# A decoder layer with sparse attention on one core: a 64-row product made one of 128 rows

## The chip, the cores and the metric

The kernel runs on one core of a Trainium2 chip. The metric is device time in microseconds for one execution. Before the change it is 919.27 us, the median of three runs (918.22 to 921.02).

## The reference

One layer of a decoder on 512 positions of width 1024: a combined input projection, a short convolution as one mixer, an attention with 16 heads (4 for keys and values, head size 64) as the other, a gated merge, and a SwiGLU block. The attention has three branches, each with keys and values of its own:

```python
p_cmp = masked_softmax(s, cmp_end[None, :] <= t[:, None])      # over 31 compressed blocks
o_cmp = einsum('bhgqn,bhnd->bhgqd', p_cmp, v_cmp)
...                                                            # selected blocks, window
o = einsum('bsch,cbshd->bshd', br_gates, o_all)                # gated sum of the three
```

The compressed branch reduces 512 positions to 31 blocks per head, kept as 32 columns (NB) of which the last is masked. Its product with the values, o_cmp, is what the change touches.

## The kernel before, in words

All matrix products use operands split in two parts (high and low, H and L), and add three products of the parts on TensorE in `mm` (lines 119 to 121). Weights come by DMA as `raw`, and ACT (line 95) and VectorE or GpSimd (line 96) split them.

The attention runs as 32 units: 8 pairs of heads (`pr`) by 4 tiles of 128 positions (`i`). The order of TensorE is the order of the program; for the other engines a planner sets the order, and `tc.high_priority` moves an instruction ahead in it. A unit goes through `slot(u)`: the scores of the next unit (`score`, matmuls of line 497), then the transposes of the compressed probabilities (`trans(u, -1)`, line 550) and of the first 128 columns of the two other branches (`trans(u, 0)`, four transposes of line 564), then two steps of filling work (`fl`, each step three matmuls of 512 columns of some other product), then `pv(u, -1, t)`, which is line 577. Then come, for each further tile j up to i, transposes, a filling step, and the products of lines 582 and 583 with the values of the two other branches; for i = 0 the scores of the unit after the next follow line 577 at once. `o_out` reads the sum (lines 591 and 594).

For the compressed branch the transposed probabilities of the two heads are 64 rows: rows 0 to 31 and 32 to 63. ACT copies the high parts into a tile (line 555, two instructions of 32 x 128), and VectorE puts the low parts into the other 32 rows of the same columns (line 557, two instructions). So one product with a stationary tile of 64 rows, `VC`, that holds the values twice, adds high and low parts. `VC` is made once, in `v_cmp` (lines 318 to 322), after the hidden layer of the compression has been transposed into `gh` and `gl`.

The tile for the transposed probabilities comes from the pool `th`, which has two buffers (`THB`); both the compressed step and each step j take one in turn. The low parts of the steps j go to `tl`, also two buffers (lines 567 and 568).

Of the kernel before, what the change touches and what calls it, by code (L numbers as in the profile page):

```python
# [8 lines left out]
F32R = mybir.dt.float32r  # L9
# [4 lines left out]
P = 128  # L14
S = 512
# [5 lines left out]
KVH = 4  # L21
NB = 32
# [9 lines left out]
def f(ap):  # L32
    return ap.bitcast(F32)

PTB = 5
THB = 2
# [10 lines left out]
def body(tc, a):  # L47
    with tc.manual_schedule(engines={mybir.EngineType.PE}):
        trace(tc, a)


def trace(tc, a):
    nc = tc.nc
    es = ExitStack()

    def pool(stack, **kw):
        return stack.enter_context(tc.tile_pool(**kw))
# [59 lines left out]
    def mm(ps, lhs, rhs, first, last):  # L117

        nc.tensor.matmul(ps, lhs[0], rhs[0], start=first, stop=False)  # L119
        nc.tensor.matmul(ps, lhs[0], rhs[1], start=False, stop=False)  # L120
        nc.tensor.matmul(ps, lhs[1], rhs[0], start=False, stop=last)  # L121
# [18 lines left out]
    kvp = pool(kvst, name="kvp", bufs=1, side="left")  # L140
# [4 lines left out]
        KH[ct] = kp.tile([P, 2, KC], F32R, name=f"KH{ct}")  # L145
        KL[ct] = kp.tile([P, 2, KC], F32R, name=f"KL{ct}")
    VT = kvp.tile([P, NT, 2, KVH, P], F32R, name="VT")
    VC = kvp.tile([2 * NB, KVH, P], F32R, name="VC")

    pst = ExitStack()  # L150
    ps1 = pool(pst, name="ps1", bufs=1, space=PSUM)
# [4 lines left out]
    def tp_tile():  # L156
        return ps1.tile([P, S], F32, name="tp", bufs=2)
# [4 lines left out]
    def av_tile():  # L162
        return ps1.tile([P, S], F32, name="av")

    oyst = ExitStack()
    oyp = pool(oyst, name="oyp", bufs=1, side="right")
# [20 lines left out]
    for k in range(KD):  # L187
# [10 lines left out]
        if 3 <= k < 3 + NT:  # L198
            t = k - 3
# [109 lines left out]
    def v_cmp(gT, w):  # L309
        ps = tp_tile()  # L310
        o = ps[:, 0:HD]
        for c in range(2):
            cc = slice(c * P, (c + 1) * P)
            wc_ = slice(c * HD, (c + 1) * HD)
            mm(o, (gT[0][:, cc], gT[1][:, cc]), (w[0][:, wc_], w[1][:, wc_]), c == 0, c == 1)
        for g in range(KVH):
            src = o[g * NB:(g + 1) * NB]
            nc.scalar.activation(VC[0:NB, g, 0:HD], src, AF.Copy, scale=0.5)
            nc.vector.scalar_tensor_tensor(VC[0:NB, g, HD:P], in0=src, scalar=0.5,
                                           in1=f(VC[0:NB, g, 0:HD]), op0=ALU.mult,  # L320
                                           op1=ALU.subtract)
        nc.vector.tensor_copy(VC[NB:2 * NB], f(VC[0:NB]))

    vps = {}

    def v_proj(br, kh):
# [145 lines left out]

    units = [(pr, i) for pr in range(8) for i in range(NT)]
    U = {}

    def scores(u):
        pr, i = units[u]
        g = pr // 2
        q = Q[pr]
        qs = slice(i * P, (i + 1) * P)  # L480
        w = (i + 1) * P
        ncol = NB + 2 * w
        b0 = S - NB - 2 * P
        pieces = [(0, 288)]
        c0 = 288
        while c0 < ncol:
            n = min(512, ncol - c0)
            pieces.append((c0, n))
            c0 += n
        U[u] = dict(pts=[], nms=[], w=w,  # L490
                    pc=ap_.tile([P, 2, NB], F32, name="pc", bufs=3))
        for h in range(2):
            ps = sc_tile()
            for c0, n in pieces:
                o = ps[:, b0 + c0:b0 + c0 + n]
                for j, kk in enumerate((KH, KL)):
                    nc.tensor.matmul(o, q[:, h, qs], kk[g // 2][:, g % 2, c0:c0 + n],  # L497
                                     start=(j == 0), stop=(j == 1))

            nr = nrs8[:, i:i + 1]  # L500
            pt = ap_.tile([P, 2 * S], F32, name="pt", bufs=PTB)
            nm = ap_.tile([P, 3], F32, name="nm", bufs=4)
            sv = ps[:, S - 2 * P:S - 2 * P + 2 * w].rearrange("p (j b c) -> p b j c", b=2, c=P)
            nc.vector.tensor_tensor_reduce(
                out=U[u]["pc"][:, h], in0=ps[:, b0:b0 + NB], in1=cmsk[:, i], scale=nr,
                scalar=TOP, op0=ALU.add, op1=ALU.min, accum_out=nm[:, 0:1])
            for b in range(2):
                r0 = b * S
                nc.vector.tensor_tensor_reduce(  # L509
                    out=pt[:, r0:r0 + w].rearrange("p (j c) -> p j c", c=P),  # L510
                    in0=sv[:, b], in1=tri[:, NT - 1 - i:NT], scale=nr, scalar=TOP,
                    op0=ALU.add, op1=ALU.min, accum_out=nm[:, b + 1:b + 2])
            U[u]["pts"].append(pt)
            U[u]["nms"].append(nm)
            yield

    def expo(u, h):
        pr, i = units[u]
        if h == 0:
            U[u]["sm"] = ap_.tile([P, 2, 3], F32, name="sm", bufs=3)  # L520
        pt, nm = U[u]["pts"][h], U[u]["nms"][h]
        for b in range(3):
            s = U[u]["pc"][:, h] if b == 0 else pt[:, (b - 1) * S:(b - 1) * S + U[u]["w"]]
            nc.scalar.activation(s, s, AF.Exp,  # L524
                                 scale=-1.0, bias=nm[:, b:b + 1],
                                 accum_out=U[u]["sm"][:, h, b:b + 1])
# [17 lines left out]
    def trans(u, j):  # L544
        pts = U[u]["pts"]
        tp = tp_tile()
        th = ap_.tile([P, S], F32R, name="th", bufs=THB)
        if j < 0:

            nc.tensor.transpose(tp[0:2 * NB, 0:P], U[u]["pc"].rearrange("p h n -> p (h n)"), ident)  # L550
            with tc.high_priority(PRI):
                rows = [slice(0, NB), slice(NB, 2 * NB)]
                cols = [slice(0, P), slice(P, 2 * P)]
                for h in range(2):
                    nc.scalar.activation(th[rows[h], cols[h]], tp[rows[h], 0:P], AF.Copy)
                for h in range(2):
                    nc.vector.tensor_tensor(th[rows[1 - h], cols[h]], tp[rows[h], 0:P],
                                            f(th[rows[h], cols[h]]), op=ALU.subtract)
            return th, None
        tl = ap_.tile([P, S], F32R, name="tl", bufs=THB)  # L560
        for b in range(2):
            for h in range(2):
                r0 = b * S + j * P
                nc.tensor.transpose(tp[:, (2 * b + h) * P:(2 * b + h + 1) * P],  # L564
                                    pts[h][:, r0:r0 + P], ident)
        with tc.high_priority(PRI):
            nc.scalar.activation(th, tp, AF.Copy)  # L567
            nc.vector.tensor_tensor(tl, tp, f(th), op=ALU.subtract)  # L568
        return th, tl

    def pv(u, j, t):
        pr, i = units[u]
        g = pr // 2
        if j < 0:
            U[u]["av"] = av_tile()[:, 0:256]
            av = U[u]["av"]
            nc.tensor.matmul(av, VC[:, g], t[0][0:2 * NB, 0:256], start=True, stop=False)  # L577
            return
        av = U[u]["av"]
        for b in range(2):  # L580
            bs = slice(b * 256, (b + 1) * 256)
            nc.tensor.matmul(av, VT[:, j, b, g], t[0][:, bs], start=False, stop=False)  # L582
            nc.tensor.matmul(av, VT[:, j, b, g], t[1][:, bs], start=False,  # L583
                             stop=(j == i and b == 1))
# [16 lines left out]
    ap_ = pool(ast, name="ap", bufs=2, side="right", reuse_waits="tile")  # L601
# [89 lines left out]
    def score(u, h):  # L691
        if u >= NU:
            return
        if h == 0:
            SC[u] = scores(u)
        next(SC[u])

    def slot(u):
# [11 lines left out]
        score(u + 1, 1)  # L710
        fl(F0[i])
        t = trans(u, -1)
        tn = trans(u, 0)
        if u + 1 < NU:
            expo(u + 1, 1)
        fl(F1[i])
        pv(u, -1, t)
        for j in range(1, i + 1):
            t, tn = tn, trans(u, j)
            fl(1)  # L720
            pv(u, j - 1, t)
            if j == 1:
                score(u + 2, 0)
# [4 lines left out]
        if u + 2 < NU:  # L728
            expo(u + 2, 0)
        fl(left)  # L730
        pv(u, i, tn)
        o_out(u)

# [6 lines left out]
    gvT = gelu_T(gv)  # L740
    fill.step(3)
    v_cmp(gvT, w2v)
    score(1, 0)
    expo(1, 0)
    fill.step(PRE)
# [332 lines left out]
```

## Time and profile before

| | before |
|---|---|
| median of three runs | 919.27 us (918.22 to 921.02) |
| profiled execution | 917.53 us, its span 915.7 us |
| TensorE matmul, busy | 898.8 us, 98% of the span |
| TensorE weight load, busy | 760.2 us, 83% |
| VectorE, busy | 515.5 us, 56% |
| ACT, busy | 426.3 us, 47% |

Busy time of TensorE is not a measure of its pace: matmuls overlap, so that 0.39 us of a 512-column matmul are followed by the next after 0.23. Weight loads (PEld) are separate rows, and normally run beside the matmul before them. What a product costs is read from the start of one matmul to the start of the next.

### The profile page before, as it was taken

How to read it: one execution, taken by the hardware profiler on the slowest of the kernel's cores; microseconds unless marked ns; L12 is line 12 of the kernel's file. 1: busy time of each engine (PE TensorE's matmuls, PEld its weight loads, DVE VectorE, ACT ScalarE, POOL GpSimd, SP SyncE). 2: the span in 40 equal slices, each digit the busy share in tenths (PEclk: the TensorE clock that was granted, in tenths of full speed). 3: DMA queues.
4: the chain of work that ended last, by engine and by line, in shares of the span. 5: the costliest groups of instructions: out<-in, count | busy, mean ns of one | idle time of the engine just before them, and what ended most of it. 6: DMA issues, size and time to landing. Idle time of an engine off the chain costs nothing.

```text
span 915.7 us, 12776 instructions
## 1 busy us (share of the span) xinstructions
PE 898.8 (98%) x4757; PEld 760.2 (83%) x4757; DVE 515.5 (56%) x1217; ACT 426.3 (47%) x936; POOL 119.6 (13%) x79
## 2 busy tenths in 40 slices
PE   9889999999999999999999999999999999999996
PEld 7789788888888888878888999888888888888885
DVE  4896788888888788775455452333333333223223
ACT  6446776767767777664333522332223222212212
POOL 1000424232242222330000300000000000000100
PEclk9999999999999999999999999999999999999999
DMA  9244511211112111114523700223333323332212
GB/s 313 70 119 162 161 47 50 67 47 53 65 46 71 47 52 65 47 64 150 178 92 97 235 16 24 93 92 92 100 108 92 92 93 103 102 94 92 93 47 92
DMA packets 26270, 85.14 MB, mean 93 GB/s; under 512 B 3424, under 2 KB 3680, under 8 KB 26208
## 3 DMA queue, kind: packets, MB, share of 16 engines
q1 hardware_dynamic: 24912, 82.78, 28.5%
q10 hardware_dynamic: 1296, 1.55, 0.5%
q8 instruction: 37, 0.61, 0.3%
q14 instruction: 25, 0.20, 0.1%
HBM read 82.23 MB, written 2.10 MB: 92 GB/s over the span
## 4 chain that ended last, share of the span: by engine, by line
PE 88%; DVE 6%; DMA 2%; ACT 2%; issue 1%; SPq 0%; POOL 0%; POOLq 0%; ACTq 0%; DVEq 0%
PE acc L119 24%; PE acc L121 24%; PE acc L120 24%; PE sc L497 4%; PE tp L564 4%; PE av L582 2%; PE av L583 2%; DVE blk L249 2%; DVE wl L96 1%; PE av L577 1%; DMA w2kr<-w2k 1%; DMA raw<-wk 1%; ACT wh L95 1%; DMA xT<-xT 0%; DMA xt<-x 0%
## 5 line engine op out<-in xcount | busy, mean ns | idle before, releaser
L95 ACT ACTIVATE wh<-raw 128x1024 fp32r<-128x1024 f32 (+2 forms) x143 | 144.6, 1013 | 314.4 <-PE acc L120 117.0
L119 PE MATMUL acc<-nH,wh 128*128 128x512 f32 x656 | 262.3, 400 | 0.0
L121 PE MATMUL acc<-nH,wl 128*128 128x512 f32 x656 | 256.1, 390 | 0.0
L120 PE MATMUL acc<-nL,wh 128*128 128x512 f32 x656 | 256.1, 390 | 0.0
L96 DVE TENSOR_TENSOR wl<-raw,wh 128x1024 fp32r<-128x1024 f32 (+2 forms) x107 | 123.4, 1154 | 170.1 <-ACT wh L95 170.0
L121 PEld LDWEIGHTS acc<-nH,wl 128*128 128x128 f32 x656 | 123.1, 188 | 26.8 <-POOL wl L96 0.4
L119 PEld LDWEIGHTS acc<-nH,wh 128*128 128x128 f32 x656 | 123.4, 188 | 21.4
L120 PEld LDWEIGHTS acc<-nL,wh 128*128 128x128 f32 x656 | 123.5, 188 | 21.2
L96 POOL TENSOR_TENSOR wl<-raw,wh 128x1024 fp32r<-128x1024 f32 x36 | 86.6, 2407 | 236.7 <-DVE pt L540 96.4
L121 PE MATMUL acc<-wh,aL 128*128 128x512 f32 (+1 forms) x198 | 73.4, 371 | 0.0
L119 PE MATMUL acc<-wh,aH 128*128 128x512 f32 (+1 forms) x198 | 73.4, 371 | 0.0
L120 PE MATMUL acc<-wl,aH 128*128 128x512 f32 (+1 forms) x198 | 73.4, 370 | 0.0
L524 ACT ACTIVATE pt<-pt,nm 128x128 f32<-128x128 f32 (+3 forms) x128 | 70.7, 554 | 2.6 <-DVE nm L509 2.0
L509 DVE CUSTOM_DVE_ANT_0 pt<-sc,tri,nrs 128x128 f32<-128x128 f32 (+3 forms) x128 | 65.4, 545 | 0.1
L568 DVE TENSOR_TENSOR tl<-tp,th 128x512 fp32r<-128x512 f32 x80 | 55.1, 689 | 13.0 <-ACT th L567 11.3
L915 DVE TENSOR_TENSOR sg<-acc,sg 128x512 f32<-128x512 f32 x22 | 15.2, 691 | 81.0 <-PE acc L121 81.0
L567 ACT ACTIVATE th<-tp 128x512 fp32r<-128x512 f32 x80 | 47.4, 592 | 13.2 <-PE tp L564 12.1
L564 PE MATMUL tp<-ident,pt 128*128 128x128 f32 x320 | 49.7, 277 | 0.1
L961 POOL TENSOR_TENSOR h<-h,gfin 128x512 f32<-128x512 f32 x4 | 6.0, 1542 | 299.1 <-ACT jk L943 299.1
L120 PEld LDWEIGHTS acc<-wl,aH 128*128 128x128 f32 x198 | 37.3, 188 | 7.1
L119 PEld LDWEIGHTS acc<-wh,aH 128*128 128x128 f32 x198 | 37.3, 188 | 7.1
L121 PEld LDWEIGHTS acc<-wh,aL 128*128 128x128 f32 x198 | 37.3, 188 | 7.0
(229 smaller groups left out, 1496.9 us busy)
## 6 DMA issues: line engine op xcount, KB each, us to landing
raw<-wg SPq DMA_DIRECT2D x22, 512.0 KB, 3.5
raw<-wu SPq DMA_DIRECT2D x22, 512.0 KB, 3.5
raw<-wd SPq DMA_DIRECT2D x22, 512.0 KB, 3.5
raw<-wcv SPq DMA_DIRECT2D x12, 512.0 KB, 3.6
raw<-wq SPq DMA_DIRECT2D x8, 512.0 KB, 3.6
raw<-w SPq DMA_DIRECT2D x8, 512.0 KB, 3.5
raw<-wgc SPq DMA_DIRECT2D x8, 512.0 KB, 3.5
raw<-wga SPq DMA_DIRECT2D x8, 512.0 KB, 3.5
```

The costliest lines, as they stand in the source:

```text
L95: nc.scalar.activation(h[:, :n], raw[:, :n], AF.Copy)
L96: ins = (eng or nc.gpsimd).tensor_tensor(l[:, :n], raw[:, :n], f(h[:, :n]), op=ALU.subtract)
L119: nc.tensor.matmul(ps, lhs[0], rhs[0], start=first, stop=False)
L120: nc.tensor.matmul(ps, lhs[0], rhs[1], start=False, stop=False)
L121: nc.tensor.matmul(ps, lhs[1], rhs[0], start=False, stop=last)
L249: nc.vector.tensor_tensor(blk[lp * HD:(lp + 1) * HD, :, 2 * ct + hp, 0:NB - 1], src, pos, op=ALU.add)
L497: nc.tensor.matmul(o, q[:, h, qs], kk[g // 2][:, g % 2, c0:c0 + n], start=(j == 0), stop=(j == 1))
L509: nc.vector.tensor_tensor_reduce(out=pt[:, r0:r0 + w].rearrange("p (j c) -> p j c", c=P), in0=sv[:, b], in1=tri[:, NT - 1 - i:NT], scale=n ...
L524: nc.scalar.activation(s, s, AF.Exp, scale=-1.0, bias=nm[:, b:b + 1], accum_out=U[u]["sm"][:, h, b:b + 1])
L564: nc.tensor.transpose(tp[:, (2 * b + h) * P:(2 * b + h + 1) * P], pts[h][:, r0:r0 + P], ident)
L567: nc.scalar.activation(th, tp, AF.Copy)
L568: nc.vector.tensor_tensor(tl, tp, f(th), op=ALU.subtract)
```

## The change

`VC` gets 128 rows, of which the lower 64 are filled with zeros once. The transposed compressed probabilities go to one 128 x 256 tile for all units, `tc0`, instead of a `th` buffer; it takes the place of `gh` in its pool once `v_cmp` has used that, and its lower 64 rows are filled with zeros once, too. The product of line 577 takes all 128 rows of both. The transposes and the four copies into rows 0 to 63 are as they were.

```diff
-    VC = kvp.tile([2 * NB, KVH, P], F32R, name="VC")
+    VC = kvp.tile([P, KVH, P], F32R, name="VC")
...
         nc.vector.tensor_copy(VC[NB:2 * NB], f(VC[0:NB]))
+        nc.vector.memset(f(VC[2 * NB:P]), 0.0)
...
+    tc0 = []
...
     def trans(u, j):
         pts = U[u]["pts"]
         tp = tp_tile()
-        th = ap_.tile([P, S], F32R, name="th", bufs=THB)
         if j < 0:
+            th = tc0[0]
...
             return th, None
+        th = ap_.tile([P, S], F32R, name="th", bufs=THB)
...
-            nc.tensor.matmul(av, VC[:, g], t[0][0:2 * NB, 0:256], start=True, stop=False)
+            nc.tensor.matmul(av, VC[:, g], t[0], start=True, stop=False)
...
     v_cmp(gvT, w2v)
+    tc0.append(oyp.tile([P, 256], F32R, name="gh"))
+    nc.vector.memset(f(tc0[0][2 * NB:P]), 0.0)
     score(1, 0)
```

## Rows read from the trace of the kernel before

**Rows 1.** The page, the chain that ended last: shares of the span by engine.
```profile
PE 88%; DVE 6%; DMA 2%; ACT 2%; issue 1%; SPq 0%; POOL 0%; POOLq 0%; ACTq 0%; DVEq 0%
```

**Rows 2.** Groups by form, weight loads: busy us, mean ns, idle us before, releasers.
```profile
L577 PEld LDWEIGHTS av<-th,VC 64*128 64x128 f32 x32 | 5.9, 183 | 12.4 <-ACT pt L524 5.0 <-ACT th L567 3.8 <-issue 2.6
```

**Rows 3.** Timeline of 301 to 304 us: start us, us, engine, line, operation.
```profile
301.65 0.28 PE L583 MATMUL av<-tl,VT 128*128 128x256 f32 x1
301.76 0.30 PE L497 MATMUL sc<-KH,q 128*128 128x288 f32 x1
301.90 0.29 PE L497 MATMUL sc<-KL,q 128*128 128x288 f32 x1
...
302.73 0.39 PE L121 MATMUL acc<-yH,wl 128*128 128x512 f32 x1
302.73 0.11 PEld L550 LDWEIGHTS tp<-ident,pc 128*64 128x64 f32 x1
302.96 0.27 PE L550 MATMUL tp<-ident,pc 128*64 128x128 f32 x1
...
303.07 0.60 PE L564 MATMUL tp<-ident,pt 128*128 128x128 f32 x4
...
303.39 0.19 PEld L119 LDWEIGHTS acc<-yH,wh 128*128 128x128 f32 x1
303.42 0.48 PE L119 MATMUL acc<-yH,wh 128*128 128x512 f32 x1
...
303.74 0.40 PE L120 MATMUL acc<-yL,wh 128*128 128x512 f32 x1
```

**Rows 4.** Timeline around line 577 of a unit with i = 3.
```profile
370.25 0.58 DVE L557 TENSOR_TENSOR th<-tp,th 32x128 fp32r<-32x128 f32 x2
...
371.01 0.40 PE L121 MATMUL acc<-nH,wl 128*128 128x512 f32 x1
...
371.33 0.18 PEld L577 LDWEIGHTS av<-th,VC 64*128 64x128 f32 x1 [0.37 <-issue]
...
371.65 0.66 PE L564 MATMUL tp<-ident,pt 128*128 128x128 f32 x4
...
372.06 0.48 PE L119 MATMUL acc<-nH,wh 128*128 128x512 f32 x1
```

**Rows 5.** The same for a unit with i = 0.
```profile
304.29 0.57 DVE L557 TENSOR_TENSOR th<-tp,th 32x128 fp32r<-32x128 f32 x2 [0.23 <-ACT th L555]
...
304.67 0.40 PE L121 MATMUL acc<-nH,wl 128*128 128x512 f32 x1
...
305.00 0.18 PEld L577 LDWEIGHTS av<-th,VC 64*128 64x128 f32 x1 [0.37 <-ACT th L567]
...
305.31 0.40 PE L497 MATMUL sc<-KH,q 128*128 128x288 f32 x1
...
305.55 0.29 PE L497 MATMUL sc<-KL,q 128*128 128x288 f32 x1
```

**Rows 6.** The same for the last unit, i = 3.
```profile
410.74 0.58 DVE L557 TENSOR_TENSOR th<-tp,th 32x128 fp32r<-32x128 f32 x2 [0.50 <-ACT th L555]
...
411.01 0.40 PE L121 MATMUL acc<-nH,wl 128*128 128x512 f32 x1
...
411.43 0.18 PEld L577 LDWEIGHTS av<-th,VC 64*128 64x128 f32 x1 [0.46 <-ACT th L567]
```

**Rows 7.** The same for a unit with i = 2.
```profile
207.09 0.58 DVE L557 TENSOR_TENSOR th<-tp,th 32x128 fp32r<-32x128 f32 x2
...
207.59 0.39 PE L121 MATMUL acc<-nH,wl 128*128 128x512 f32 x1
```

**Rows 8.** Timeline of VectorE, where VC is made and just after.
```profile
106.55 0.49 DVE L322 CAST VC<-VC 32x512 fp32r<-32x512 f32 x1
107.88 0.68 DVE L427 TENSOR_TENSOR q<-acc,q 64x512 fp32r<-64x512 f32 x1 [0.84 <-ACT q L426]
```

**Rows 9.** Busy us of each engine in four units, then granted clock, DMA share, GB/s.
```profile
151.00:190.00 39.00, 39.00 (x220) 32.34 (x218) 33.50 (x112) 27.62 (x81) 12.19 (x7) 1.00 0.18 56
```

## The prediction

> **What bounds the kernel now.** I read the chain of waits first: TensorE holds 88% of it, and no other engine more than 6% [rows 1], so whatever shortens TensorE's row of instructions in the attention part shortens the kernel, as long as the others keep up. Next I read the groups of TensorE's weight loads by form. In the attention part one line stands out: the 32 loads of line 577, the only ones of 64 rows, had 12.4 us of idle load queue before them, 0.39 us each [rows 2]. The idle time is attributed to two ACT lines and to "issue". An idle time that stays the same while its named releaser changes suggests that none of them is the cause, so I went to the timeline, to see what stands around such a load and around one of full height.
>
> In the stream without line 577 [rows 3], the load of line 550 starts with the matmul before it (both at 302.73), and matmuls start after one another at the pace of their columns: a 512-column one holds the array 0.23 us (302.73 to 302.96), the 256-column one of line 583 holds it 0.11 us (301.65 to 301.76), a 288-column one 0.14 us (301.76 to 301.90).
>
> Around line 577 this breaks [rows 4]. Its operand was complete when line 557 ended (370.25 + 0.58 = 370.83), before the preceding matmul even started (371.01). Its load could have run beside that matmul, but starts at 371.33, 0.32 after it, and the work behind line 577 starts 0.32 after that again (371.65), where 256 columns hold the array 0.11. So the array empties on the way into the 64-row product and again on the way out. A unit with i = 0 shows the same where the scores follow [rows 5]: 0.33 in, 0.31 out. Of the 32 loads 27 start 0.31 to 0.33 after the preceding matmul; the other five start about 0.11 after line 557 ended, as in [rows 6] (410.74 + 0.58 = 411.32, load at 411.43). The load therefore starts at the later of two times: the preceding matmul + 0.32, or the end of line 557 + 0.11.
>
> **The change part by part.** *The height of line 577.* With 128 rows the product has the same shape as lines 582 and 583, which stream. I take the 0.32 on both sides to go. What is late next is line 557: the wait for it stands in front of the load and stays. A load that came too late to hide shows what it costs: line 119's load starts at 303.39, the matmul behind its own starts at 303.74; 0.35 less the 0.23 of its own columns is 0.12 [rows 3]. So the new product starts to stream at the later of (preceding matmul + 0.23) and (end of line 557 + 0.11 + 0.12), and what follows comes 0.11 later. What follows also gets its usual pace back: four transposes take 0.41 to the next matmul now (371.65 to 372.06) [rows 4] against 0.35 (303.07 to 303.42) [rows 3], 0.06 each in the 24 units with i > 0; the first score matmul takes 0.24 (305.31 to 305.55) [rows 5] against 0.14, some 0.10 each in the 8 with i = 0.
>
> By the index i of the unit, 8 units each:
> - i = 0 [rows 5]: line 557 ends at 304.29 + 0.57 = 304.86, 0.19 after the preceding matmul's start (304.67). The second score matmul, now at 305.55, would start at 304.86 + 0.23 + 0.11 + 0.14 = 305.34: 0.21 saved. All eight are like this: 8 x 0.215 = 1.7 us.
> - i = 1: as the next, but line 557 ends only 0.04 to 0.05 after the preceding matmul's start (seven units; before it in one): 0.30 to 0.32 saved, and 0.36 in the one, 2.5 us.
> - i = 2 [rows 7]: line 557 ends at 207.67, 0.08 after the matmul's start (207.59): the product streams at +0.31 instead of +0.23, and some 0.27 is saved; in the one unit where line 557 is 0.80 late, 0.16. Sum 2.0 us.
> - i = 3 [rows 4]: nothing is late, 372.06 becomes 371.01 + 0.23 + 0.11 + 0.35 = 371.70: 0.36 saved in five units; in three, as in [rows 6], line 557 ends 0.27 to 0.31 after the matmul's start: 0.15. Sum 2.2 us.
>
> Together 8.5 us. The ends of this term: if the wait did not hold the load back but only the product, the 0.12 would go too, which gives 10.9 us; with no wait at all it would be 12.7 us; and if the height is not the cause, 0.
>
> Here a rule speaks against the change. The Trainium skill ("TensorE: Matmul & The Clock Gate", section "LDWEIGHTS (loading the stationary operand)") says that a load of 32 rows takes as long as one of 128, since only columns count. By that sentence alone the change is worth 0. The trace agrees about the load itself: 183 ns for 64 rows [rows 2], 0.19 us for 128 [rows 3]. But the cost measured here lies in the gap ahead of it, of which the same skill ("TensorEngine Tiling (Array Packing)", "Key Properties") says that changing the tiling mode drains the engine; by that, the gap goes. I keep both as cases.
>
> *The new buffer.* The transposed probabilities of the compressed branch go to one buffer for all units instead of a turn of the two th buffers. Line 555 of a unit must then wait until line 577 of the unit before has read it; that is some 9.5 us earlier (seven units lie between the loads at 305.00 and 371.33 [rows 4, 5]), so 0. In return the two th buffers serve the j steps alone; the wait that this takes away, line 567 of j = 1 on line 577, was always over, since TensorE runs line 577 before the transposes of j = 1. 0 as well. The planner orders ACT and VectorE and may place line 557 elsewhere; that is in the rivals.
>
> *Two fills with zeros*, once each, on VectorE near 105 to 107 us. No row shows a fill of this shape; the nearest is the copy of 32 x 512, 0.49 us [rows 8]. Between nothing and 0.49 + 0.49 = 1.0 us for both; I take 0.7. VectorE then stands idle for 0.84 us ahead of line 427 [rows 8], which hides that; without this cover at most 1 us would be lost, once. The fill of the new buffer waits until the matmuls of v_cmp have read the buffer's former content; behind it queue the scores' reductions, but line 319 in front of it waits for the same matmuls already.
>
> *What is late next.* Four units take about 38 us now, and VectorE works 33.50 of 39 us there, ACT 27.62 [rows 9]. With about 1.1 us less for four units VectorE goes from 0.86 to 0.88 of the time. It has 5.5 us of idle time in that row and follows TensorE, so I expect it to keep up. The granted clock is 1.00, the 2.4 GHz level, in that stretch and has nowhere to rise.
>
> The profiled execution took 917.53 us (915.7 of span and 1.8 around it), 1.7 below the median of the three runs shown. 917.53 - 8.5 = 909.0 against that execution; from the median it is 910.8. I name 910.
>
> **The rivals.**
> - *No change.* The 0.32 belongs to something else at line 577, such as its two waits: lines 555 on ACT and 557 on VectorE both write its operand, where lines 582 and 583 read a tile with one writer each. Against it: in [rows 4] line 557, the later of the two, had finished 0.5 before the load, and the gap behind line 577 comes without any wait of its own. Then 917.5 to 919.3, say 919. Chance 0.08.
> - *The gain is partly eaten by line 557.* VectorE is 86% busy [rows 9], so line 557 will often find it at work, and as TensorE moves ahead by 0.3 a unit, line 557 may come later relative to it. By the same sum, 0.1 later in every unit leaves 5.9 us, 0.2 leaves 2.8: 912 to 916. Chance 0.15.
> - *More than forecast.* The load goes ahead of the wait: 10.9 us, 908. For it: load and matmul are separate instructions. Against it: the five late loads, of which one is in [rows 6], start only after line 557. Chance 0.10.
> - *Slower.* With the th buffers freed, the planner places one more VectorE instruction of the size of line 427 (0.68 us [rows 8]) ahead of line 557 in every unit. TensorE, which runs in order, would stand at line 577 for it. By the same sum the gain is gone from 0.29 later on, and 0.68 later costs 12.5 us: 930 to 932. For it: nothing but the planner's order protects line 557. Against it: lines 555 and 557 keep the priority that they have, and stand ahead of lines 567 and 568 in the program. Chance 0.05.
>
> The forecast itself holds 0.62.
>
> **How the numbers follow.** The runs shown spread by 0.3% (918.22 to 921.02), about what can be told from no change. Faster by over 0.3% (below 916.5) are the forecast, the larger gain and nearly all of the partly eaten one: 0.62 + 0.10 + 0.15 = 0.87. Within: 0.08. Slower: 0.05. The range reaches from the largest gain, 12.7 from the profiled execution (905), to the partly eaten one at 0.2 later (917); it leaves out no change and slower.
>
> **What would show it.** In the changed profile the load of line 577 (a few lines further down there) has 128 rows, and most of its idle time ahead is gone: from 12.4 us to between 2 and 5. The matmuls behind it start 0.11 after it where line 557 was early, and the product takes the 0.28 us that line 583 takes in [rows 3]. All of the gain lies between 112 and 412 us; that stretch shortens by about 8.5 and nothing changes behind it. I am wrong if the new product still starts 0.3 after the preceding matmul with line 557 long over, or if line 557 ends later after that matmul's start than the 0.04 to 0.19 of most units now.

## The result, and the profile after

The changed kernel took 913.92 us (median of five runs, 913.51 to 917.84), the kernel before beside it 920.83 (918.22 to 921.90). The ratio is 0.9944, 95% interval 0.9930 to 0.9959: faster by about 5.1 us, 3.8 to 6.4. A second set of runs (e10 below) gave 0.9945. 910.0 was forecast, so the direction and the mechanism came out as forecast and 3.4 us of the 8.5 did not come.

| | before | changed |
|---|---|---|
| profiled execution | 917.53 us | 913.92 us |
| its span | 915.7 us | 912.1 us |
| preceding matmul of the first compressed product | 111.94 | 113.51 |
| the same of the second unit | 120.93 | 123.52 |
| the same of the last unit | 411.01 | 407.51 |

In the changed kernel line 577 is line 581, line 557 is 560, 555 is 558, 564 is 568, 567 and 568 are 571 and 572, 582 and 583 are 586 and 587, 497 is 500, 504 and 509 are 507 and 512, 427 and 428 are 429 and 430, 540 is 543, 591 and 594 are 595 and 598. Line numbers from here on are those of the kernel that is spoken of.

The chain that ended last, from the page of the changed kernel [rows 1]:

```profile
PE 89%; DVE 6%; ACT 3%; issue 1%; DMA 1%; POOL 0%; POOLq 0%; ACTq 0%; DVEq 0%
```

TensorE still sets the time. The weight loads of line 581, by form [rows 2]:

```profile
L581 PEld LDWEIGHTS av<-gh,VC 128*128 128x128 f32 x32 | 6.0, 187 | 11.3 <-ACT th L571 4.6 <-ACT pt L527 3.0 <-issue 2.3
```

A load of 128 rows takes 187 ns, as one of 64 took 183. The idle time ahead of it has hardly fallen, 12.4 to 11.3 us, although the kernel is faster: that sum doesn't show whether the array ran dry. The timeline does. A unit with i = 3 of the changed kernel, start and duration in us, then engine and line [rows 4]:

```profile
367.56 0.57 DVE L560 TENSOR_TENSOR gh<-tp,gh 32x128 fp32r<-32x128 f32 x2
...
368.04 0.40 PE L121 MATMUL acc<-nH,wl 128*128 128x512 f32 x1
368.25 0.19 PEld L581 LDWEIGHTS av<-gh,VC 128*128 128x128 f32 x1 [0.25 <-issue]
...
368.48 0.60 PE L568 MATMUL tp<-ident,pt 128*128 128x128 f32 x4
...
368.83 0.48 PE L119 MATMUL acc<-nH,wh 128*128 128x512 f32 x1
```

The load no longer starts 0.32 after the preceding matmul: it starts 0.12 after line 560 ended (368.13), beside the matmul. The next 512-column matmul comes 0.79 after the preceding one, not 1.05. But line 560 now ends 0.09 after that matmul's start, where line 557 ended 0.18 ahead of it. A unit with i = 0 [rows 5], and one with i = 2 [rows 7]:

```profile
302.74 0.57 DVE L560 TENSOR_TENSOR gh<-tp,gh 32x128 fp32r<-32x128 f32 x2 [0.25 <-ACT gh L558]
...
303.10 0.40 PE L121 MATMUL acc<-nH,wl 128*128 128x512 f32 x1
303.43 0.19 PEld L581 LDWEIGHTS av<-gh,VC 128*128 128x128 f32 x1 [0.38 <-ACT th L571]
...
303.65 0.30 PE L500 MATMUL sc<-KH,q 128*128 128x288 f32 x1
...
303.79 0.29 PE L500 MATMUL sc<-KL,q 128*128 128x288 f32 x1
```

```profile
207.54 0.57 DVE L560 TENSOR_TENSOR gh<-tp,gh 32x128 fp32r<-32x128 f32 x2
...
208.04 0.39 PE L121 MATMUL acc<-nH,wl 128*128 128x512 f32 x1
208.23 0.19 PEld L581 LDWEIGHTS av<-gh,VC 128*128 128x128 f32 x1 [0.23 <-ACT pt L527]
```

The load stands 0.12 behind the end of line 560 in both (303.31 and 208.11), as before it did only where line 557 was late [rows 6]. At i = 0 the second score matmul comes 0.69 after the preceding matmul instead of 0.88.

At the other end, the stretch where VC is made, answering to [rows 8] (GpSimd, VectorE and the first load of line 581):

```profile
105.92 4.76 POOL L96 TENSOR_TENSOR wl<-raw,wh 128x1024 fp32r<-128x1024 f32 x2 [3.87 <-DVE pt L543]
...
109.15 1.81 DVE L322 CAST VC<-VC 32x512 fp32r<-32x512 f32 x1
...
110.98 0.68 DVE L429 TENSOR_TENSOR q<-acc,q 64x512 fp32r<-64x512 f32 x1
...
114.32 0.58 DVE L560 TENSOR_TENSOR gh<-tp,gh 32x128 fp32r<-32x128 f32 x2 [0.85 <-ACT gh L558]
...
115.01 0.19 PEld L581 LDWEIGHTS av<-gh,VC 128*128 128x128 f32 x1 [1.53 <-ACT th L571]
```

The copy of line 322 took 1.81 us instead of 0.49 and ended at 110.96, 0.28 after GpSimd's two splits did (110.68); the 0.84 us of idle time ahead of line 427, the cover of the forecast, are gone (0.02 left), and line 560 of the first unit ends 1.39 us after the preceding matmul's start instead of 0.28.

Where the time went, read from the starts of the matmul ahead of the compressed product, unit to unit. The thirty steps from the second unit to the last, summed by the index i of the unit left and the unit reached:

| step | count | before | changed | gain | forecast |
|---|---|---|---|---|---|
| i = 0 to 1 | 7 | 60.15 | 58.88 | 1.27 | 1.5 |
| i = 1 to 2 | 8 | 78.74 | 76.39 | 2.35 | 2.5 |
| i = 2 to 3 | 8 | 75.69 | 74.48 | 1.21 | 2.0 |
| i = 3 to 0 | 7 | 75.50 | 74.24 | 1.26 | 2.0 |
| together | 30 | 290.08 | 283.99 | 6.09 | 8.0 |

So the attention gave 6.1 us instead of 8.0 in these steps, and the profiled execution had lost 2.6 us by the second unit (123.52 against 120.93), some of it run to run. From the matmul ahead of the last unit's product to the end of the span it is 504.74 us before and 504.60 in the changed kernel: the last unit's own gain, forecast at 0.15, and nothing behind it.

VectorE's share in four units answers to [rows 9]: 0.87, 33.06 of 38 us; the granted clock stays at the 2.4 GHz level.

```profile
149.00:187.00 38.00, 38.00 (x220) 32.37 (x220) 33.06 (x112) 27.07 (x77) 12.20 (x7) 1.00 0.19 56
```

### The profile page after: what moved, and what is told of

Its sections match the earlier page's. It is cut to its first block, busy times and chain, and to the rows that moved or that the text cites. A ratio compares the mean times of both kernels' runs of the same rounds, so it can differ in the third digit from the quotient of the medians.

```text
span 912.1 us, 12767 instructions
## 1 busy us (share of the span) xinstructions
PE 892.1 (98%) x4757; PEld 761.3 (83%) x4757; DVE 518.0 (57%) x1219; ACT 425.0 (47%) x936; POOL 119.1 (13%) x79
## 4 chain that ended last, share of the span: by engine, by line
PE 89%; DVE 6%; ACT 3%; issue 1%; DMA 1%; POOL 0%; POOLq 0%; ACTq 0%; DVEq 0%
PE acc L119 24%; PE acc L120 24%; PE acc L121 24%; PE sc L500 4%; PE tp L568 4%; PE av L587 2%; PE av L586 2%; DVE blk L249 2%; PE sc L119 1%; PE sc L121 1%; PE sc L120 1%; ACT wh L95 1%; PE av L581 1%; DVE wl L96 1%; DMA raw<-wq 1%
```

## The experiments

Each time is a median, each ratio is to the kernel before, run beside it on the same chip, with a 95% interval.

**e1: the product of 64 rows, all else as changed.**

```diff
-            nc.tensor.matmul(av, VC[:, g], t[0], start=True, stop=False)
+            nc.tensor.matmul(av, VC[0:2 * NB, g], t[0][0:2 * NB], start=True, stop=False)
```

> The changed kernel with its product of line 581 back at 64 rows; the buffer, its fills and the order of ACT and VectorE stay as changed. Theory (the height alone makes the gain, the buffer gives nothing): the loads of line 581 start 0.32 after the preceding matmul again, some 6 us come back, the time is 919 to 922 against 914 of the changed kernel. Rival (the gain comes from the freed th buffers): it stays at 914 to 915.

Measured: 921.62 us, 1.0020 (1.0010 to 1.0031). A unit with i = 1 of e1:

```profile
353.28 0.58 DVE L560 TENSOR_TENSOR gh<-tp,gh 32x128 fp32r<-32x128 f32 x2
...
353.82 0.40 PE L121 MATMUL acc<-yH,wl 128*128 128x512 f32 x1
354.14 0.18 PEld L581 LDWEIGHTS av<-gh,VC 64*128 64x128 f32 x1 [0.36 <-ACT pt L527]
...
354.46 0.66 PE L568 MATMUL tp<-ident,pt 128*128 128x128 f32 x4
```

The gaps are back, 0.32 in (line 560 ended at 353.86, 0.28 ahead of the load) and 0.32 out, and the thirty steps take 290.22 us, those of the kernel before. The height makes all of the gain. What is left of the change, buffer and fills, costs: line 560 of the first unit is late by 1.38 here too.

**e2: 96 rows.**

```diff
-            nc.tensor.matmul(av, VC[:, g], t[0], start=True, stop=False)
+            nc.tensor.matmul(av, VC[0:3 * NB, g], t[0][0:3 * NB], start=True, stop=False)
```

> The changed kernel with a product of 96 rows. Theory (the array empties only when a product takes another division of the rows than its neighbours, and 96 rows need the whole array): no gap, 913 to 915, the product 0.11 apart from what follows. Rival (the gap grows with the rows that are missing): half of the gain is gone, 916 to 918, and the loads start between 0.1 and 0.3 late where line 560 is early.

Measured: 915.76 us, 0.9958 (0.9944 to 0.9971); thirty steps in 284.18. A unit with i = 2:

```profile
360.58 0.57 DVE L560 TENSOR_TENSOR gh<-tp,gh 32x128 fp32r<-32x128 f32 x2
...
361.08 0.39 PE L121 MATMUL acc<-nH,wl 128*128 128x512 f32 x1
361.27 0.19 PEld L581 LDWEIGHTS av<-gh,VC 96*128 96x128 f32 x1 [0.23 <-ACT pt L527]
...
361.50 0.60 PE L568 MATMUL tp<-ident,pt 128*128 128x128 f32 x4
```

The load starts 0.12 after line 560 and 0.19 after the matmul: 96 rows stream like 128. It isn't missing rows that cost, but the 64-row form among others.

**e8: the 64-row product twice in the kernel before.**

```diff
-            nc.tensor.matmul(av, VC[:, g], t[0][0:2 * NB, 0:256], start=True, stop=False)
+            for r in range(2):
+                nc.tensor.matmul(av, VC[:, g], t[0][0:2 * NB, 0:256], start=(r == 0), stop=False)
```

> The kernel before, its 64-row product of line 577 issued twice (the second adds to the first, so the compressed branch counts double). Theory (the array empties where the height changes, not for every 64-row product): the second starts 0.11 after the first, 3.6 us in all, 923 us. Rival (each 64-row load waits for the matmul before it): the second starts 0.3 after the first, 10 us, 929 us.

Measured: 924.0 us, 1.0040 (1.0026 to 1.0053): 3.7 us for 32 more products, 0.12 each, about the 0.11 that 256 columns hold the array. A unit with i = 1:

```profile
356.21 0.40 PE L121 MATMUL acc<-yH,wl 128*128 128x512 f32 x1
356.53 0.29 PEld L578 LDWEIGHTS av<-th,VC 64*128 64x128 f32 x2 [0.36 <-ACT pt L524]
...
356.97 0.66 PE L564 MATMUL tp<-ident,pt 128*128 128x128 f32 x4
```

Two loads of 64 rows take 0.29 together, one takes 0.18, so they stand 0.11 apart, and the work behind comes 0.76 after the preceding matmul where one product makes it 0.64. The cost is paid where 128 rows change to 64 and back, on the way in and on the way out, and not per product. That is what the Trainium skill says ("TensorEngine Tiling (Array Packing)", section "Key Properties"): changing the tiling mode, not just the tile, drains the engine. The trace agrees: of the 0.64 the columns hold the array for 0.23 and 0.11, and about 0.30 are lost to the two changes.

**e3: three steps of filling work instead of two ahead of the product, so that nothing waits for line 560.**

```diff
-F1 = [2, 2, 2, 2]
+F1 = [3, 3, 3, 3]
```

> The changed kernel with three filling steps instead of two between the transposes and line 581 (the third is taken from the end of the unit). Theory (what is left of the forecast gain is the wait for line 560, 0.05 to 0.25 a unit): line 581 starts 0.23 after the preceding matmul in nearly all units, 2 to 3.5 us faster than the changed kernel, 911 to 912. Rival (VectorE is the bound behind it and takes back whatever TensorE saves): the wait moves to the low parts of a later tile, within 1 us of the changed kernel.

Measured: 917.51 us, 0.9976 (0.9966 to 0.9986). The 2 to 3.5 us did not come; it is slower than the changed kernel. The waits of TensorE's load queue and of its matmuls between 112 and 415 us (what waited, for what, us in total, times, longest):

```profile
PEld av L587 <- DVE tl L572: 4.9, 12, 0.6
...
```

```profile
PE av L587 <- DVE tl L572: 1.7, 7, 0.3
...
```

The wait at line 581 is gone in 28 of the 32 units, and another stands behind it: products of the j steps now wait for the low parts of line 572, up to 0.6 us.

**e7: e5 (below) with one filling step more behind the transposes of j = 1.**

```diff
-            fl(1)
+            fl(2 if j == 1 else 1)
```

> Both fills on GpSimd, and two filling steps instead of one between the transposes of j = 1 and the products of j = 0. Theory (in units with i = 2 some 0.12 is given back because the low parts of a tile, line 572, come late): the steps between units i = 2 and i = 3 shorten by 0.1 more, 0.5 to 1 us faster than with one step. Rival (VectorE's order sets the length of these units): no faster than with one step, the wait turns up at another line.

Measured: 915.99 us, 0.9950 (0.9937 to 0.9964), against 0.9936 for e5: no gain. The wait of line 587 for line 572 in units with i = 2, at which it was aimed, is gone, but line 560 of i = 2 now ends 0.24 to 0.32 after the preceding matmul in seven units, and the steps from i = 2 to 3 give nothing any more (75.74 against 75.69 before). Moving filling work about moves the wait.

**e4: the copy of line 322 on ACT.**

```diff
-        nc.vector.tensor_copy(VC[NB:2 * NB], f(VC[0:NB]))
+        nc.scalar.activation(VC[NB:2 * NB], f(VC[0:NB]), AF.Copy)
```

> The changed kernel with the copy of VC's rows 0 to 31 to 32 to 63 (line 322) on ACT instead of VectorE. Theory (in the changed kernel that copy took 1.81 us instead of 0.49 beside a split on GpSimd, which made line 560 of the first unit 1.1 us late): the first unit's wait falls from 1.4 to about 0.3 and the kernel is 0.5 to 1.3 us faster. Rival (the copy's length is hidden, the first unit waits for something else): no change beyond 0.3 us.

Measured: 914.74 us, 0.9948 (0.9933 to 0.9963), no gain. Line 560 of the first unit is still 1.24 late: ACT does the copy at 111.19, behind it stands line 428, and VectorE's line 429 waits 2.12 us for that. In the second unit line 560 is 1.05 late. Not the copy alone is late but the order around it.

**e5 and e6: the fills on GpSimd.** In e5 both, in e6 that of VC alone; VC is filled at the start, where GpSimd builds masks. With both there, ACT and VectorE have the written order of the kernel before.

```diff
+    nc.gpsimd.memset(f(VC[2 * NB:P]), 0.0)
...
-        nc.vector.memset(f(VC[2 * NB:P]), 0.0)
...
-    nc.vector.memset(f(tc0[0][2 * NB:P]), 0.0)
+    nc.gpsimd.memset(f(tc0[0][2 * NB:P]), 0.0)
```

> The changed kernel with both fills on GpSimd instead of VectorE. ACT and VectorE then get the order of the kernel before, instruction for instruction. Theory (the fill of the new buffer on VectorE made the planner put a split of weights ahead of VC's copies, which starts GpSimd earlier and lets VectorE's copy of line 322 run against it; with the fill of VC ahead of the warm-up this is the 2 us that are lost before the first unit): line 560 of the first unit ends 0.3 after the preceding matmul instead of 1.4, 1 to 2.5 us faster than the changed kernel, 912 to 913.5. Rival (the loss comes from the buffer itself or from chance): 914 to 915.

> The changed kernel with only the fill of VC on GpSimd. Theory: the first matmul starts at 1.95 as before instead of 2.59, at most 0.6 us faster than the changed kernel, and the first unit's wait of 1.4 us stays: 913.5 to 914.5. Rival (the fill of VC is the whole loss): as the run with both fills there.

Measured: e5 914.63 us, 0.9936 (0.9923 to 0.9948); e6 915.64, 0.9951 (0.9938 to 0.9963). Thirty steps: 284.10 and 284.06. In e5 the first matmul starts at 1.94 as in the kernel before (changed: 2.59, behind the fill of VC), and the first unit is as punctual as before:

```profile
115.07 0.57 DVE L560 TENSOR_TENSOR gh<-tp,gh 32x128 fp32r<-32x128 f32 x2 [0.85 <-ACT gh L558]
115.77 0.19 PEld L581 LDWEIGHTS av<-gh,VC 128*128 128x128 f32 x1 [0.45 <-ACT th L571]
```

The load queue had stood idle for 0.45 us, not 1.53. The time forecast for e5, 912 to 913.5, did not come: 914.63 is what its rival said. In e6 the first matmul starts at 1.94 too, but the kernel is no faster than the changed one, and the first unit is 1.64 late: the fill of the transposed tile, 0.27 us of work at 105.80 in the changed kernel, shifts the order in which ACT takes a weight split and the copies of VC, and this brings GpSimd's two splits next to each other beside line 322. e5 is the best version that leaves nothing out, but its interval overlaps that of the changed kernel.

**e9: e5 with 64 rows, that is the buffer alone.**

> The changed kernel with both fills on GpSimd and the product back at 64 rows: the buffer alone, with the order of ACT and VectorE of the kernel before. Theory (the buffer costs nothing, all that the change loses outside the height comes from the fills on VectorE and the order that follows from them): the time of the kernel before, within 0.5 us. Rival (the buffer itself costs): 1 to 2 us slower than before, as with the fills on VectorE.

Measured: 920.07 us, 0.9998 (0.9989 to 1.0008). The buffer costs nothing. Against e1, which has 64 rows too and the fills on VectorE, that puts the fills at 0.22%, 2.0 us; the intervals allow from next to nothing to 3.9.

**e10: the changed kernel once more.**

> The changed kernel once more, beside the others. Theory: 914 to 915; the run with the fills on GpSimd was 0.5 to 1.3 us faster than this if its gain at the first unit is real.

Measured: 915.45 us, 0.9945 (0.9932 to 0.9958), thirty steps in 284.09, the first unit 1.63 late. By the ratios e5 is 0.8 us faster, which is within the intervals.

**e11 and e12: less work on VectorE.** The scaling of the second branch's probabilities left out, in e5 (e11) and in the kernel before (e12).

```diff
-        for b in range(2):
+        for b in range(1):
```

> Both fills on GpSimd, and the scaling of the second branch's probabilities (half of line 543, some 0.5 us of VectorE's work a unit) left out, so its part of the output is not normalised. Theory (VectorE's order behind TensorE makes line 560 later and takes back part of what the height gives): line 560 ends earlier relative to the preceding matmul, at i = 3 by 0.1 or more, and 1.5 to 3 us are gained over the run with the fills on GpSimd, 911.5 to 913. Rival (ACT or the waits themselves set it): no change, 914 to 915.

> The same scaling left out of the kernel before: how much VectorE's work costs there. Theory (before the change the empty array at the 64-row product covers VectorE's delay): within 0.8 us of the kernel before. Rival (VectorE bounds the units in both kernels alike): the same 1.5 to 3 us are gained.

Measured: e11 913.96 us, 0.9925 (0.9906 to 0.9943); e12 919.16, 0.9988 (0.9978 to 0.9999). Both gain about 1 us by the ratios, e11 against e5 with overlapping intervals, and line 560 at i = 3 stays 0.06 to 0.07 behind the matmul in most units. My theory that VectorE's load as a whole makes line 560 late fell.

What makes it late is seen in the times from one line 557 or 560 to the next. The kernel before, VectorE, lines 557 of a unit with i = 2 and of the next:

```profile
168.66 0.58 DVE L557 TENSOR_TENSOR th<-tp,th 32x128 fp32r<-32x128 f32 x2
...
177.82 0.57 DVE L557 TENSOR_TENSOR th<-tp,th 32x128 fp32r<-32x128 f32 x2
```

The changed kernel, the same two units, with some of what lies between:

```profile
170.05 0.58 DVE L560 TENSOR_TENSOR gh<-tp,gh 32x128 fp32r<-32x128 f32 x2
171.24 0.69 DVE L572 TENSOR_TENSOR tl<-tp,th 128x512 fp32r<-128x512 f32 x1 [0.61 <-ACT th L571]
...
172.51 0.88 DVE L543 TENSOR_SCALAR pt<-pt,fac 128x512 f32<-128x512 f32 x2
173.30 0.69 DVE L572 TENSOR_TENSOR tl<-tp,th 128x512 fp32r<-128x512 f32 x1
174.02 0.68 DVE L429 TENSOR_TENSOR q<-acc,q 64x512 fp32r<-64x512 f32 x1
...
175.44 0.69 DVE L572 TENSOR_TENSOR tl<-tp,th 128x512 fp32r<-128x512 f32 x1
...
176.76 0.88 DVE L543 TENSOR_SCALAR pt<-pt,fac 128x512 f32<-128x512 f32 x2
...
177.96 0.58 DVE L598 TENSOR_TENSOR oT<-av,ol 64x128 f32<-64x128 f32 x2
...
179.22 0.58 DVE L560 TENSOR_TENSOR gh<-tp,gh 32x128 fp32r<-32x128 f32 x2
```

It is 9.16 us before and 9.17 after, while TensorE's step between the same units went from 9.36 to 9.20. Between the two lines 560 VectorE has hardly a gap; the only long one, 0.61, is a wait for ACT. So this stretch is a chain of VectorE and ACT with a length of its own, and a faster TensorE meets its end later. It doesn't run through the second line 543: beside that (176.76 to 177.64) ACT does three instructions of line 527 and then line 595 (177.55), for which line 598 waits. e11 had left out the pair beside the chain; the first pair, at 172.51, stands on it.

**e13 and e14: all four scalings left out,** in e5 and in the kernel before.

```diff
-        nc.vector.tensor_tensor(pc, pc, fac[:, :, 0:1].to_broadcast([P, 2, NB]), op=ALU.mult)
-        for b in range(2):
+        ins = nc.vector.tensor_tensor(pc, pc, fac[:, :, 0:1].to_broadcast([P, 2, NB]), op=ALU.mult)
+        for b in ():
```

> The kernel of e5 without the scaling of the probabilities of both branches (line 543 is left out, 4 instructions a unit; e11 left out two of them). Theory: from line 560 of a unit with i = 2 to line 560 of the next unit, VectorE and ACT form one closed chain that TensorE does not set. It took 9.15 to 9.18 us before the change and 9.17 to 9.21 after it, so its end falls later against a TensorE that has become faster: 0.12 ahead of the preceding matmul became 0.07 behind it. e11 left out the two scalings that stand beside three ACT instructions, so it could not shorten it; the other two stand on it: 0.79 us between VectorE's line 539 and line 572. ACT lets it gain at most about 0.24 of that. I expect 8.95 to 9.0 from line 560 to line 560, line 560 of i = 3 ending 0.05 to 0.15 ahead of the preceding matmul again, the step from i = 2 to i = 3 at 9.03 to 9.1 instead of 9.20 (a gain of 0.25 to 0.33 over the kernel before, where the changed kernel has 0.15), and the time 1 us or more below e11, about 913. Rival: the lateness is fixed by the order of the transposes and the filling steps on TensorE itself, so line 560 still ends 0.05 to 0.07 behind the matmul and the step stays at 9.20; the time as e11.

> The kernel before with the same four scalings left out (line 540 there). Theory of the closed chain: before the change line 557 of i = 3 ends 0.10 to 0.18 ahead of the preceding matmul and the drain hides it, so a shorter chain gives nothing there: the step from i = 2 to i = 3 stays at 9.36, and the time gains the 1 us that e12 gained, at most 1.5: 918 to 919. Rival: the scalings cost TensorE time in both kernels alike: the step falls by as much as in e13.

Measured: e13 912.63 us, 0.9921 (0.9897 to 0.9946); e14 918.70, 0.9990 (0.9977 to 1.0004). e13, the same pair of units:

```profile
171.12 0.58 DVE L560 TENSOR_TENSOR gh<-tp,gh 32x128 fp32r<-32x128 f32 x2
...
180.07 0.58 DVE L560 TENSOR_TENSOR gh<-tp,gh 32x128 fp32r<-32x128 f32 x2
...
180.77 0.19 PEld L581 LDWEIGHTS av<-gh,VC 128*128 128x128 f32 x1
```

The chain is 8.95 us long, line 560 ends 0.06 ahead of the preceding matmul again, the load follows it by 0.12, early enough to hide beside that matmul, and the step takes 9.11. In e14 the same omission leaves that step at 9.36: there the drain hid the chain.

| thirty steps | e14 | e13 | gain | changed kernel's |
|---|---|---|---|---|
| i = 0 to 1 | 60.20 | 58.93 | 1.27 | 1.27 |
| i = 1 to 2 | 78.82 | 76.97 | 1.85 | 2.35 |
| i = 2 to 3 | 75.41 | 73.36 | 2.05 | 1.21 |
| i = 3 to 0 | 75.50 | 73.50 | 2.00 | 1.26 |
| together | 289.93 | 282.76 | 7.17 | 6.09 |

With the chain shortened both steps beside i = 3 give what was forecast, 2.0 each. (The 1.85 has one step of the second unit in it, where line 560 is 0.47 late.) The times of e11 and e13 can't be told apart by their intervals; the steps can.

## Why the prediction was wrong in size

*The drain: right.* Undoing the height alone brings the old steps back to 0.15 us in 290 (e1), and 96 rows are as good as 128 (e2). Of the rivals, "no change" is excluded by the measured interval, and the sentence of the Trainium skill ("TensorE: Matmul & The Clock Gate", section "LDWEIGHTS (loading the stationary operand)") that only columns count is right of the load's own duration (183 and 187 ns) and says nothing of the gap.

*The wait in front of the load: right.* Loads now start 0.11 to 0.12 after line 560, so "more than forecast" fell. But the mark that I set for it, an idle sum of 2 to 5 us at the load queue, was wrong by my own sum: a load that waits for line 560 stands idle whether the array runs dry or not.

*The buffer at 0: right* (e9).

*The step that failed inside the units: VectorE, "I expect it to keep up", and with it "i = 3 [rows 4]: nothing is late".* The prediction held line 557's distance from the preceding matmul constant, although at i = 3 that distance is the difference of two lengths, VectorE's 9.16 and TensorE's 9.36, of which the change shortens one. The lateness went from 0.10 to 0.18 ahead to 0.05 to 0.10 behind in five units, and from 0.27 to 0.46 and 0.49 behind in two, whose following steps lose 0.05 and 0.08 instead of gaining.

The same chain is late at a second place, which the prediction put at nothing. In four units with i = 2 the products of j = 1 now wait for line 572. The kernel before, and the changed kernel:

```profile
172.96 0.28 PE L583 MATMUL av<-tl,VT 128*128 128x256 f32 x1
173.08 0.28 PE L582 MATMUL av<-th,VT 128*128 128x256 f32 x1
```

```profile
174.04 0.19 PEld L587 LDWEIGHTS av<-tl,VT 128*128 128x128 f32 x1
174.09 0.34 PE L587 MATMUL av<-tl,VT 128*128 128x256 f32 x1
...
174.27 0.28 PE L586 MATMUL av<-th,VT 128*128 128x256 f32 x1
```

The load of line 587 starts 0.05 after line 572 ended (173.30 + 0.69 = 173.99), and the next product comes 0.18 after this one instead of 0.12. The four units lose 0.06 to 0.09 each in this way, and none do in e13. In the last unit with i = 2 line 560 itself is 1.12 late instead of 0.81, and the step loses 0.17 instead of gaining 0.16; with the scalings left out it is 0.51 and 0.50 late (e13, e14).

The mean share of VectorE, 33.50 of 39 us [rows 9], and "it has 5.5 us of idle time in that row" were the wrong measure: the idle time lies in other steps. Between lines 557 the steps from i = 3 to 0 take about 11.07 before and 10.63 after, and those from 1 to 2 about 9.86 and 9.56; only those from 2 to 3 keep their length. So 1.5 of the 8.0 us went, about half in the steps from 2 to 3 and half in those from 3 to 0, and e13 gets them back. The other 0.4 are small sizes: 0.18 a step instead of 0.215 after i = 0, 0.29 instead of 0.31 after i = 1.

*The second step that failed: the two fills.* "VectorE then stands idle for 0.84 us ahead of line 427, which hides that." Their length was forecast well, 0.48 and 0.27 us against 0.7 together, but neither cost what it took. That of VC ran at 1.59 us, since its tile was free, ahead of the instruction for which the first matmul waits, and the first matmul starts 0.64 us later; that this reaches the end is not shown, since e6 without it is no faster. That of the transposed tile changed the order of ACT and VectorE, and from the first unit to the second it takes about 1 us more: 10.0 in the changed kernel and 10.3 in e6 and e10, against 9.0 before, 8.9 in e5 and 9.0 in e9. The two fills together are the difference between e1 and e9, 2.0 us with a wide interval. From e9 to e5, both with the fills on GpSimd, the height gives 0.62%, 5.7 us, near the 6.1 of the steps.

*The sum.* 8.5 forecast; 1.9 less in the thirty steps, some 1 to 2 lost at the fills: 4.6 to 5.6, measured 5.1. The rival "partly eaten by line 557", with its 912 to 916, is what happened, and in part for the reason it gave (line 557 comes later relative to a TensorE that moves ahead), though not because VectorE is busy in general, and not at line 557 alone.

What stays open: how what was lost ahead of the second unit divides between the two fills and the spread of single executions, which is larger than either: the matmul ahead of the first compressed product stands at 113.51 in one profile of the changed kernel and at 116.31 in the other (e10).

## What to carry to other kernels

A 64-row product inside a stream of full ones empties the array on the way in and on the way out, about 0.3 us a product here. A 96-row one did not, and no other height was tried. Zero rows up to the height of the neighbours buy that back, and the fills should go where no order hangs on them. Before a wait is taken to keep its distance, measure the stretch on the other engine from one such instruction to the next: where it is as long as TensorE's step is going to be, it is the next bound, however idle that engine is on average. Idle time at a load queue is no measure of an idle array; starts of matmuls are.

## What the runs showed of the hardware that was not expected

Instructions of VectorE from SBUF to SBUF stretch beside a split on GpSimd. Line 277 took 0.29 us before and 1.05 in the changed kernel, and 2.52 in e4, where it started at 99.75 and ended at 102.27, 0.15 after GpSimd's (97.37 and 4.75 long):

```profile
97.37 4.75 POOL L96 TENSOR_TENSOR wl<-raw,wh 128x1024 fp32r<-128x1024 f32 x2 [46.56 <-DVE wl L96]
...
99.75 2.52 DVE L277 TENSOR_SCALAR gt<-gt 128x256 f32<-128x256 f32 x1 [0.24 <-ACT gt L276]
```

Line 322, 1.81 instead of 0.49, is the same case: it ended 0.28 after GpSimd's splits. In the kernel before, too, it began beside a split (below) and ended 0.28 after that, at 107.04, so that its 0.49 were in part a wait [rows 8]:

```profile
104.34 2.42 POOL L96 TENSOR_TENSOR wl<-raw,wh 128x1024 fp32r<-128x1024 f32 x1 [3.80 <-DVE VC L319]
```

Line 319, which reads PSUM, kept its 0.21 to 0.23 beside the same splits. The Trainium skill ("SBUF — State Buffer", section "SBUF: two separate sides") says that VectorE and GpSimd share a port pair: whichever starts first, a GpSimd instruction or a VectorE instruction in a two-port mode or with two SBUF inputs, holds it for its whole length while the other waits. The ends of lines 277 and 322, 0.15 and 0.28 after GpSimd's, agree with such a wait; in which mode the two ran no run here shows.
